# A two-layer diffusion block on one core: attention tiles in their own buffer list, the next layer's first norm chunks ahead of the context adds, and modulation bias and norm factors once per four pairs

## The chip, the cores and the metric

The kernel runs on one core of a Trainium2 chip. The metric is the device time of one execution in microseconds (us), the median of several runs; lower is better. The core has five engines with queues of their own: TensorE (PE) multiplies matrices into PSUM, VectorE (DVE) and ScalarE (ACT) do element-wise work, GpSimd (POOL) a part of it, and SyncE (SP) issues nearly all transfers from HBM.

## The reference, cut to what matters

Two layers work on 512 latent tokens (x) and 256 context tokens (h), both 1024 wide. Every layer computes a modulation from the condition vectors, normalises, projects once into four groups of mixers, projects back, and runs a SwiGLU network. `mod_c` is the same modulation from the context's condition vector.

```python
for l in range(DEPTH):                                    # DEPTH = 2
    mod = split(silu(c) @ w_mod[l] + b_mod[l], 6)         # shift1, scale1, gate1, shift2, scale2, gate2
    hn = rms_norm(h, g_norm1[l]) * (1 + mod_c[1]) + mod_c[0]
    xn = rms_norm(x, g_norm1[l]) * (1 + scale1) + shift1
    p = xn @ w_in[l]                                      # q, k, v, Fourier, convolution, pooling columns
    attn = attend(q, concat(kc, k), concat(vc, v))        # context keys come from hn
    mix = concat(attn, fourier, conv, pool) @ w_out[l]
    x = x + gate1 * mix
    xn = rms_norm(x, g_norm2[l]) * (1 + scale2) + shift2
    a, g = split(xn @ w_ffn_in[l], 2)
    x = x + gate2 * (silu(a) * g) @ w_ffn_out[l]
    # the context stream h does the same, in the first layer alone
```

## The kernel before

Activations stand transposed: `x[k]` is chunk k of the 1024 features (128 partitions) by 768 tokens, LAT (columns 0 to 511) and CTX (512 to 767). Every number is cut into a rounded high part and a rest, so that a product takes three matmuls (`mm3`: high by high, high by rest, rest by high). The cut of a weight is an ACT copy (`hi`) and a subtraction (`sub_lo`) on the engine in `lo_eng`: POOL in the mixing phase, DVE in the SwiGLU phase.

Buffers come from lists. `W` is a list of 14 tiles of 4 KB for a partition (pool `wp`): a weight of 512 KB takes three, the raw tile, `hi` and `lo`. `AL` is a list of 28 tiles of 768 numbers (`alp`), for activations. PSUM has three lists of two (`pt`, `pf`, `pb`). A tile's transfer or first write waits until an old tile of its list has had its last reader.

The order of the instructions on an engine is not that of the source. It is fixed when the program is built, by a planner that simulates the program; what stands earlier in the source goes first among what is ready in that simulation. On the chip an engine keeps the order that it was given.

The stages, with the names that the change touches:

- `mix_phase(l)`: `norm.apply` makes the chunks of the first norm (a DVE scale `xt`, an ACT shift to `xnh`, a DVE rest `xnl`), four `wq` loads feed the q, k, v projection; then 24 attention tiles in layer 0 (16 in layer 1), with the other projections, pooling, Fourier and convolution work threaded between them by `fill`, and convolution taps on DVE (`run`, L669). `make_qT` writes `qst` and `qT` (from AL), `Tile.flip` transposes a tile's probabilities into `pt_`, which two heads share (one or two W tiles).
- `mod_pairs` is a generator that runs beside the attention tiles (q 8 to 23, that is chunks 16 to 47) and, for layer 1's q 0 to 7, beside layer 0's SwiGLU. For a pair of chunks it multiplies (`mod`), copies (`me`), transposes (`mods`), reduces (L343), adds the bias (L344) and, for the scale chunks, makes the norm factor `a` (L324, `scaled_gain`).
- Out-projection at the end of `mix_phase`: eight `wo` loads; the first four are held for two passes, the last four for the first and the second part of the tokens. Meanwhile the second norm's first part is made.
- `ffn(l)`: 22 columns of 128. Layer 0 works with the seven products of a scheme of Strassen's kind (`fast`, weights by `load_ff`: two raw tiles and seven cut ones of W), after `fast_first`, which does columns 0 and 1 directly: `z` 0 is the first 384 tokens, `z` 1 the rest, whose operands `A.second` makes meanwhile. Layer 1 uses plain products (`first_step`, `ag`). `out_step` is the second matrix with its add to `x` (L1362). In the last step of layer 0 the order in the source is LAT's two `out_step`s, LAT's `n1.rstd`, CTX's two `out_step`s, CTX's `n1.rstd`; then the modulation generator is run to its end, and layer 1 begins.

Of the kernel before, what the change touches and what calls it, by code (L numbers as in the profile page):

```python
# [19 lines left out]
P = 128  # L20
# [30 lines left out]
def kernel(ctx: ExitStack, tc: tile.TileContext, xT, ctxT, vec, cst, dft,  # L51
# [8 lines left out]
    wp = ctx.enter_context(tc.tile_pool(name="wp", bufs=14))  # L60
# [16 lines left out]
    def W(name, dt=F32R):  # L77
        return wp.tile([P, 1024], dt, tag="w", name=name)

    def RAW(name):  # L80
        return W(name, F32)
# [147 lines left out]
    def load_ff(l, c):  # L229

        raws = []
        for o in (0, DFF):
            raw = RAW("ff")
            nc.sync.dma_start(out=raw.rearrange("p (a b) -> p a b", b=P), in_=rows(w_ffn_in[l][:, o + P * c:o + P * c + P]))
            raws.append(raw)
        a1, a2, g1, g2 = (r[:, 512 * i:512 * i + 512] for r in raws for i in range(2))
        ops = {}

        def cut(nm, full):
            w = ops[nm] = W("f" + nm)  # L240
            hi, lo = w[:, 0:512], w[:, 512:1024]
            act.copy(out=hi, in_=full)  # L242
            sub_lo(lo_eng[0], lo, full, hi)

        def comb(out, in0, in1, op):
            sum_eng[0].tensor_tensor(out=out, in0=in0, in1=in1, op=op)  # L246
        cut("a11", a1)
        cut("a12", a2)
        cut("a22", g2)
        comb(g2, g1, g2, ALU.add)  # L250
        comb(g1, a1, g1, ALU.subtract)
        comb(a1, g2, a1, ALU.subtract)
        comb(a2, a2, a1, ALU.subtract)
        for nm, full in (("s2", a1), ("s3", g1), ("s1", g2), ("s4", a2)):
            cut(nm, full)
        return ops
# [69 lines left out]
    def mod_pairs(l, q0, q1, mix=True):  # L326
# [11 lines left out]
        def finish(q, me):  # L338
            ps = PF("mods")
            for c in range(2):  # L340
                tr(ps[:, 128 * c:128 * c + 128], me[:, 128 * c:128 * c + 128], ident)
            m2 = modT[l][:, 2 * q:2 * q + 2, :]
            dve.tensor_reduce(out=m2, in_=ps[:, 0:256].rearrange("p (c g w) -> p c w g", c=2, g=4)[:, :, 0:2, :], axis=AX.X, op=ALU.add)  # L343
            dve.tensor_tensor(out=m2, in0=m2, in1=vcol(l, V_BM + 2 * q, 2).unsqueeze(2).to_broadcast([P, 2, 2]), op=ALU.add)  # L344
            if q // 4 in (1, 4):
                scaled_gain(l, q // 12, 2 * q % 8, 2 * q % 8 + 2)
# [252 lines left out]
    def mix_phase(l, norm, A, filler):  # L599
# [363 lines left out]
        def make_qT(i):  # L963
            j, o = qpos(i)
            st = AL("qst")
            src = qsb[j][:, o:o + 256].rearrange("p (h d) -> p h d", h=4)
            sv = lambda a: a[:, 0:512].rearrange("p (h s d) -> p h s d", h=4, s=2)
            act.copy(out=sv(st)[:, :, 0, :], in_=src)
            dve.tensor_tensor(out=sv(st)[:, :, 1, :], in0=src, in1=sv(b32(st[:, 0:512]))[:, :, 0, :], op=ALU.subtract)
            ps = PT("qT")  # L970
            for h in range(NQ):
                tr(ps[:, P * h:P * h + P], b32(st[:, P * h:P * h + P]), ident)
            qTs[i] = AL("qT")
            act.copy(out=qTs[i][:, 0:512], in_=ps[:, 0:512])

        class Tile:
# [24 lines left out]
            def flip(self, pt_):  # L1001

                e = self.h % 2
                for j, (c0, n) in enumerate(((0, 2),) if self.nk == 2 else ((0, 4), (4, 2))):
# [3 lines left out]
                    dst = pt_[j][:, 512 * e:512 * e + P * n]  # L1008
# [4 lines left out]
                if not e:  # L1013
                    return
                po = PT("pv")
                for c in range(self.nk):
                    v = vsb[:, P * (self.k0 + c) + 64 * self.kv:P * (self.k0 + c) + 64 * self.kv + 64]
                    for g in range(2):
                        o = 512 * g + P * (c % 4)
                        mm(po[64 * g:64 * g + 64, 0:P], v, pt_[c // 4][:, o:o + P], start=c == 0, stop=c == self.nk - 1,  # L1020
                           tile_position=(0, 64 * g))
# [87 lines left out]
        pt_ = None  # L1109
        for i in range(len(tiles) + 2):  # L1110
# [4 lines left out]
            if i >= 2:  # L1115
                t = tiles[i - 2]
                if t.h % 2 == 0:
                    pt_ = [W("pt", F32) for _ in range(1 if t.nk == 2 else 2)]
                t.flip(pt_)
# [84 lines left out]
    def ffn(l, norm, first, second, A, filler):  # L1204
# [22 lines left out]
        def fast_first():  # L1227
# [4 lines left out]
            for z in range(2):  # L1232
# [6 lines left out]
                for k in range(KD):  # L1239
                    if z:  # L1240
                        nm = ("b12", "b22")[k // 4]
                    else:
                        nm = ("b11", "b21")[k // 4]
                    xh, xl = A.h(nm, k % 4), A.l(nm, k % 4)
                    for i in range(4):
                        mm3(out[i], ws[i][0][:, P * k:P * k + P], ws[i][1][:, P * k:P * k + P], xh, xl, k == 0, k == KD - 1)
# [42 lines left out]
        def fast_steps():  # L1289
            fast_first()  # L1290
            for s in range(1, ns):
# [7 lines left out]
                if fin:  # L1299
                    wl = [need(("fo", l, NF - 2)), need(("fo", l, NF - 1))]  # L1300
                    for sl, st in streams:
                        out_step(s - 1, sl, st, wo, False)
                        out_step(s, sl, st, wl, True)
                        if not last:
                            n1.rstd(sl)
                else:
# [4 lines left out]
                next(filler, None)  # L1311

# [59 lines left out]
        ns = NF // 2  # L1372
        if FAST[l]:
            fast_steps()
        else:
            first_step()
# [29 lines left out]
        return n1  # L1406
# [21 lines left out]
    for l in range(DEPTH):  # L1428
        nxt = mix_phase(l, norm, A, mod_pairs(l, 8, 24))
        filler = mod_pairs(1, 0, 8, False) if l == 0 else iter(())  # L1430
        norm, A = ffn(l, *nxt, filler), None
# [82 lines left out]
```

## Time and profile before

| | us |
|---|---|
| median of three runs | 1476.47 |
| their lowest and highest | 1474.70, 1476.76 |
| the profiled execution: its own time | 1474.25 |
| its span, first to last instruction | 1472.5 |

The profiled execution lies 2.22 us under the median of the runs, and 1.75 us of its time lie around its span. The columns of a view stand in the line above its rows; times of a row are us from the span's start unless it says otherwise. "PE ssq L161 <- POOL acca L437" reads: a matmul that writes `ssq`, issued by line 161, waited for POOL's write of `acca` in line 437. Line 161 is a helper that issues all matmuls, line 105 one that issues all subtractions of cuts.

### The profile page before, as it was taken

The page shows a single profiled execution, that of the slowest core. Times are in us where ns is not written, and L with a number is a line of the kernel's source. Part 1 is how long each engine was busy: PE and PEld are TensorE (multiplying, and loading weights), DVE is VectorE, ACT ScalarE, POOL GpSimd, SP SyncE. Part 2 cuts the span into 40 slices and gives each one's busy share as a digit, 9 for nine tenths or more (in the row PEclk, how much of TensorE's full clock was granted, in tenths as well). Part 3 has the DMA queues.
Part 4 walks back from the last instruction along what each step waited for, and adds up shares of the span by engine and source line. Part 5 has one row for each costly group of instructions (what it writes and reads, how often), then busy time and mean ns, then how long its engine had stood idle before and what let it go on. Part 6 is the DMA issues. An engine that isn't in the chain of part 4 may idle for free.

```text
span 1472.5 us, 20702 instructions
## 1 busy us (share of the span) xinstructions
PE 1417.3 (96%) x8298; PEld 1217.2 (83%) x8298; DVE 945.2 (64%) x1572; ACT 600.2 (41%) x1035; POOL 199.3 (14%) x161
## 2 busy tenths in 40 slices
PE   7999988999999999999999989999899999999998
PEld 4787766998998999999999968776698888888887
DVE  3569577247986778686877777866545545444444
ACT  4457656436533233332332345666544322222220
POOL 2526420420000000000000035430240000000000
PEclk9999989999999999999999999999999999999999
DMA  9525433320323133222322233356442323333231
GB/s 297 164 87 165 157 110 107 109 71 26 104 70 103 54 91 114 87 68 76 115 86 58 92 111 92 117 169 211 127 114 80 108 86 90 111 101 100 89 98 57
DMA packets 192928, 157.35 MB, mean 107 GB/s; under 512 B 6464, under 2 KB 179520, under 8 KB 192832
## 3 DMA queue, kind: packets, MB, share of 16 engines
q1 hardware_dynamic: 192544, 155.34, 34.4%
q8 instruction: 65, 1.06, 0.3%
q10 hardware_dynamic: 288, 0.69, 0.1%
q14 instruction: 31, 0.25, 0.1%
HBM read 151.81 MB, written 4.19 MB: 106 GB/s over the span
## 4 chain that ended last, share of the span: by engine, by line
PE 83%; DVE 7%; ACT 4%; DMA 4%; issue 1%; POOL 1%; SPq 0%; ACTq 0%; DVEq 0%; POOLq 0%
PE ag L161 35%; PE fo L161 20%; PE wo L161 6%; PE qkv L161 4%; PE cv L161 3%; PE agl L161 3%; PE mod L161 3%; DVE run L669 3%; PE u L161 2%; PE ssq L161 1%; PE S L161 1%; DMA wm<-in_w_mod_dram 1%; PE pv L161 1%; PE PT L167 1%; PE cc L161 1%
## 5 line engine op out<-in xcount | busy, mean ns | idle before, releaser
L1362 DVE SCALAR_TENSOR_TENSOR x<-fo,mod,x 128x512 f32<-128x512 f32 (+1 forms) x264 | 170.7, 657 | 81.0 <-PE fo L161 80.5
L161 PE MATMUL fo<-hl,foh 128*128 128x512 f32 (+1 forms) x528 | 187.7, 356 | 0.0
L161 PE MATMUL fo<-hh,fol 128*128 128x512 f32 (+1 forms) x528 | 187.4, 356 | 0.0
L161 PE MATMUL fo<-hh,foh 128*128 128x512 f32 (+1 forms) x528 | 185.5, 358 | 1.9 <-DVE x L1362 1.4
L161 PE MATMUL ag<-t,fs 128*128 128x384 f32 x720 | 136.6, 336 | 0.9 <-DVE hg L1266 0.9
L161 PEld LDWEIGHTS ag<-t,fs 128*128 128x128 f32 x720 | 125.0, 188 | 6.4 <-issue 1.6
L161 PEld LDWEIGHTS fo<-hh,foh 128*128 128x128 f32 x528 | 99.0, 188 | 16.1 <-DVE x L1362 1.8
L161 PEld LDWEIGHTS fo<-hh,fol 128*128 128x128 f32 x528 | 99.2, 188 | 15.1 <-issue 0.2
L161 PEld LDWEIGHTS fo<-hl,foh 128*128 128x128 f32 x528 | 99.2, 188 | 14.7 <-issue 0.7
L182 ACT CAST foh<-fo 128x1024 fp32r<-128x1024 f32 x44 | 46.2, 1050 | 146.0 <-DMA fo<-in_w_ffn_out_dram 146.0
L161 PE MATMUL ag<-b,fa 128*128 128x384 f32 x480 | 92.6, 336 | 1.5 <-DVE ht L1216 1.5
L105 DVE TENSOR_TENSOR fol<-fo,foh 128x1024 fp32r<-128x1024 f32 x44 | 53.8, 1222 | 54.1 <-ACT foh L182 41.9
L669 DVE SCALAR_TENSOR_TENSOR run<-glu,vt,run 128x512 f32<-128x512 f32 (+1 forms) x98 | 87.0, 887 | 1.0
L161 PEld LDWEIGHTS ag<-b,fa 128*128 128x128 f32 x480 | 83.4, 188 | 3.4 <-DVE ht L1216 1.8
L242 ACT CAST fs<-ff 128x512 fp32r<-128x512 f32 x80 | 45.4, 620 | 75.0 <-DVE ff L246 53.0
L437 POOL TENSOR_TENSOR acca<-acca,sq 128x512 f32<-128x512 f32 (+1 forms) x4 | 4.5, 1117 | 523.8 <-ACT sq L436 523.8
L161 PE MATMUL wo<-mxh,wol 128*128 128x384 f32 (+2 forms) x224 | 73.7, 330 | 0.0
L161 PE MATMUL wo<-mxl,woh 128*128 128x384 f32 (+2 forms) x224 | 73.5, 329 | 0.0
L161 PE MATMUL wo<-mxh,woh 128*128 128x384 f32 (+2 forms) x224 | 73.5, 331 | 0.1
L161 PE MATMUL ag<-xfh,fah 128*128 128x512 f32 (+1 forms) x192 | 71.3, 376 | 1.2 <-ACT xfh L465 1.2
L161 PE MATMUL ag<-xfl,fah 128*128 128x512 f32 (+1 forms) x192 | 71.6, 373 | 0.8 <-DVE xfl L466 0.8
L242 ACT CAST fa<-ff 128x512 fp32r<-128x512 f32 x60 | 35.6, 619 | 90.2 <-PE ag L161 51.7
(319 smaller groups left out, 3308.1 us busy)
## 6 DMA issues: line engine op xcount, KB each, us to landing
wm<-in_w_mod_dram SPq DMA_DIRECT2D x64, 512.0 KB, 4.4
fo<-in_w_ffn_out_dram SPq DMA_DIRECT2D x44, 512.0 KB, 3.3
ff<-in_w_ffn_in_dram SPq DMA_DIRECT2D x40, 512.0 KB, 4.7
fa<-in_w_ffn_in_dram SPq DMA_DIRECT2D x24, 512.0 KB, 4.4
fg<-in_w_ffn_in_dram SPq DMA_DIRECT2D x24, 512.0 KB, 3.9
wm<-in_w_mod_dram SPq DMA_DIRECT2D x40, 256.0 KB, 5.3
wo<-in_w_out_dram SPq DMA_DIRECT2D x16, 512.0 KB, 4.8
wm<-in_w_mod_dram SPq DMA_DIRECT2D x16, 384.0 KB, 3.3
```

What stands on the lines that cost most here:

```text
L105: eng.tensor_tensor(out=out, in0=full, in1=b32(hi), op=ALU.subtract)
L161: i = last_pe[0] = pe.matmul(*a, **kw)
L167: i = last_pe[0] = pe.transpose(*a)
L182: act.copy(out=hi[:, :n], in_=raw[:, :n])
L242: act.copy(out=hi, in_=full)
L437: eng.tensor_tensor(out=a, in0=a, in1=t[:, sl], op=ALU.add)
L669: yield dve.scalar_tensor_tensor(out=cacc[b][:, :cwid] if j == CONVW - 1 else run, in0=glu[b][:, j:j + cwid], scalar=tap(b, j), in1=cacc[b ...
L1362: dve.scalar_tensor_tensor(out=x[m][:, sl], in0=ps[:, :n], scalar=modT[l][:, 40 + m, st:st + 1], in1=x[m][:, sl], op0=ALU.mult, op1=ALU.add)
```

## The change

1. W has 11 tiles instead of 14. A new list `AT` has four tiles of 768 numbers, which is the same memory. From it come `qst`, `qT`, and a tile `pt` for each head (before: `pt_` from W for two heads, `qst` and `qT` from AL), and in `load_ff` the raw weights, now four loads of 512 numbers a partition instead of two of 1024.
2. The bias add and the norm factor of the modulation are done once for eight chunks (every fourth q), not for each pair.
3. In `fast_first`, `z` 1 does the four outputs in two passes of two over all eight k, not all four for each k.
4. In the last step of layer 0, behind LAT's `n1.rstd` and ahead of CTX's `out_step`s in the source, the modulation generator is run to its end, and layer 1's first norm is applied to chunks 0 and 1 of LAT.

```diff
-    wp = ctx.enter_context(tc.tile_pool(name="wp", bufs=14))
+    wp = ctx.enter_context(tc.tile_pool(name="wp", bufs=11))
+    tp = ctx.enter_context(tc.tile_pool(name="tp", bufs=4))
...
+    def AT(name, dt=F32):
+        return tp.tile([P, T], dt, tag="at", name=name)
...
-        for o in (0, DFF):
-            raw = RAW("ff")
-            nc.sync.dma_start(out=raw.rearrange("p (a b) -> p a b", b=P), in_=rows(w_ffn_in[l][:, o + P * c:o + P * c + P]))
+        for o, i in ((0, 0), (0, 1), (DFF, 1), (DFF, 0)):
+            raw = AT("ff")[:, 0:512]
+            nc.sync.dma_start(out=raw.rearrange("p (a b) -> p a b", b=P), in_=rows(w_ffn_in[l][512 * i:512 * i + 512, o + P * c:o + P * c + P]))
             raws.append(raw)
-        a1, a2, g1, g2 = (r[:, 512 * i:512 * i + 512] for r in raws for i in range(2))
+        a1, a2, g2, g1 = raws
...
-            m2 = modT[l][:, 2 * q:2 * q + 2, :]
-            dve.tensor_reduce(out=m2, in_=ps[:, 0:256].rearrange("p (c g w) -> p c w g", c=2, g=4)[:, :, 0:2, :], axis=AX.X, op=ALU.add)
-            dve.tensor_tensor(out=m2, in0=m2, in1=vcol(l, V_BM + 2 * q, 2).unsqueeze(2).to_broadcast([P, 2, 2]), op=ALU.add)
-            if q // 4 in (1, 4):
-                scaled_gain(l, q // 12, 2 * q % 8, 2 * q % 8 + 2)
+            dve.tensor_reduce(out=modT[l][:, 2 * q:2 * q + 2, :], in_=ps[:, 0:256].rearrange("p (c g w) -> p c w g", c=2, g=4)[:, :, 0:2, :],
+                              axis=AX.X, op=ALU.add)
+            if q % 4 == 3:
+                v = modT[l][:, 2 * q - 6:2 * q + 2, :]
+                dve.tensor_tensor(out=v, in0=v, in1=vcol(l, V_BM + 2 * q - 6, KD).unsqueeze(2).to_broadcast([P, KD, 2]), op=ALU.add)
+                if q // 4 in (1, 4):
+                    scaled_gain(l, q // 12, 0, KD)
...
-            st = AL("qst")
+            st = AT("qst", F32R)
...
-            qTs[i] = AL("qT")
+            qTs[i] = AT("qT", F32R)
...
-            def flip(self, pt_):
+            def flip(self, pair):
...
+                self.pt = AT("pt")
...
-                    dst = pt_[j][:, 512 * e:512 * e + P * n]
+                    dst = self.pt[:, P * c0:P * (c0 + n)]
...
-                for k in range(KD):
...
-                    for i in range(4):
-                        mm3(out[i], ws[i][0][:, P * k:P * k + P], ws[i][1][:, P * k:P * k + P], xh, xl, k == 0, k == KD - 1)
+                for pair in ((0, 1), (2, 3)) if z else ((0, 1, 2, 3),):
+                    for k in range(KD):
+                        nm = f"b{1 + k // 4}{1 + z}"
+                        for i in pair:
+                            mm3(out[i], ws[i][0][:, P * k:P * k + P], ws[i][1][:, P * k:P * k + P], A.h(nm, k % 4), A.l(nm, k % 4),
+                                k == 0, k == KD - 1)
...
                         if not last:
                             n1.rstd(sl)
+                            if st == 0:
+                                for _ in filler:
+                                    pass
+                                nxt = Acts("xn")
+                                for k in range(2):
+                                    n1.apply(l + 1, 0, k, sl, st, nxt)
...
-        norm, A = ffn(l, *nxt, filler), None
+        norm, A = ffn(l, *nxt, filler)
```

## Rows read from the trace of the kernel before

**Rows 1.** The page's first part: busy us (share of the span) and instructions.

```profile
PE 1417.3 (96%) x8298; PEld 1217.2 (83%) x8298; DVE 945.2 (64%) x1572; ACT 600.2 (41%) x1035; POOL 199.3 (14%) x161
```

**Rows 2.** Busy time by stretch: engines (instructions), granted PE clock, DMA share, GB/s.

```profile
160.00:262.00 102.00, 88.44 (x704) 69.39 (x705) 66.38 (x143) 61.14 (x137) 13.43 (x14) 0.90 0.39 119
389.00:837.00 448.00, 447.15 (x2615) 416.74 (x2614) 345.59 (x605) 143.86 (x254) 0.00 (x0) 1.00 0.28 85
1139.00:1446.00 307.00, 307.00 (x1345) 252.16 (x1344) 145.03 (x167) 81.02 (x95) 0.00 (x0) 1.00 0.31 95
```

**Rows 3.** PE's waits, 837 to 890: total us, times, longest us.

```profile
PE ssq L161 <- POOL acca L437: 4.0, 1, 4.0
PE fo L161 <- DVE x L1362: 1.4, 1, 1.4
```

**Rows 4.** PE's waits, 340 to 390.

```profile
PE ag L161 <- DVE b L105: 1.7, 2, 1.0
PE ag L161 <- DVE ht L1216: 1.5, 1, 1.5
```

**Rows 5.** The chain that ended last, 100 to 270: start, us, what.

```profile
126.44 1.60 DVE mod L344
131.14 1.70 DVE mod L344
153.53 1.58 DVE mod L344
```

**Rows 6.** Busy time of L344's bias adds alone, on DVE, 75 to 262.

```profile
75.00:262.00 187.00, 8.57 (x16) 0.95 0.39 123
```

**Rows 7.** Timeline near 131, DVE and then POOL: start, us, instruction.

```profile
130.10 1.04 DVE L669 SCALAR_TENSOR_TENSOR run<-glu,vt,run 128x783 f32<-128x783 f32 x1
131.05 1.79 DVE L344 TENSOR_TENSOR mod<-mod,vt 128x4 f32<-128x4 f32 x1
...
130.95 1.88 POOL L685 TENSOR_TENSOR ca<-ca,prod 128x783 f32<-128x783 f32 x1 [0.57 <-ACT prod L684]
```

**Rows 8.** The chain that ended last, 925 to 1110 (layer 1's mixing phase).

```profile
957.96 0.80 DVE mod L344
```

**Rows 9.** The chain that ended last, 837 to 893.

```profile
878.46 3.68 PE ssq L161 x8
...
882.36 5.47 PE qkv L161 x24
```

**Rows 10.** Timeline at the layers' boundary, DVE and then POOL.

```profile
864.85 3.35 DVE L451 RECIPROCAL R<-R 128x512 f32<-128x512 f32 x1
868.12 1.95 DVE L1362 SCALAR_TENSOR_TENSOR x<-fo,mod,x 128x256 f32<-128x256 f32 x5
...
877.74 1.87 DVE L463 SCALAR_TENSOR_TENSOR xt<-x,a,R 128x512 f32<-128x512 f32 x2
879.86 3.18 DVE L466 SCALAR_TENSOR_TENSOR xnl<-xt,mod,xnh 128x512 fp32r<-128x512 f32 x2 [0.24 <-ACT xnh L465]
...
869.14 2.40 POOL L105 TENSOR_TENSOR wql<-wq,wqh 128x1024 fp32r<-128x1024 f32 x1 [12.12 <-PE fo L161]
...
879.28 2.55 POOL L105 TENSOR_TENSOR wcl<-wc,wch 128x1024 fp32r<-128x1024 f32 x1 [0.88 <-ACT wch L182]
```

**Rows 11.** All engines' busy time in one stretch, columns as in the second group.

```profile
878.60:882.00 3.40, 3.40 (x9) 2.58 (x10) 3.15 (x3) 1.84 (x3) 2.55 (x1) 0.50 0.00 0
```

**Rows 12.** The chain that ended last, 318 to 392.

```profile
364.01 16.40 PE ag L161 x92
```

**Rows 13.** The chain that ended last, 1060 to 1125.

```profile
1093.71 5.31 DMA fg<-in_w_ffn_in_dram
...
1099.09 1.06 ACT fgh L182
...
1100.18 1.23 DVE fgl L105
```

**Rows 14.** SP's waits, 290 to 390.

```profile
SPq L188 <- PE wo L161: 31.3, 3, 23.0
```

More of the change, by code (lines that the diff above doesn't have):

```diff
@@ L999, in soft @@
                 act.activation(out=pr[:, 0:kw], in_=pr[:, 0:kw], func=AF.Copy, scale=st[:, 2:3])
-            def flip(self, pt_):
-                e = self.h % 2
+            def flip(self, pair):
+                self.pt = AT("pt")
                 for j, (c0, n) in enumerate(((0, 2),) if self.nk == 2 else ((0, 4), (4, 2))):
@@ L1012, in flip @@
                         act.copy(out=dst, in_=pt[:, 0:P * n])
-                if not e:
+                if self.h % 2 == 0:
                     return
@@ L1018, in flip @@
                     for g in range(2):
-                        o = 512 * g + P * (c % 4)
-                        mm(po[64 * g:64 * g + 64, 0:P], v, pt_[c // 4][:, o:o + P], start=c == 0, stop=c == self.nk - 1,
+                        mm(po[64 * g:64 * g + 64, 0:P], v, pair[g].pt[:, P * c:P * c + P], start=c == 0, stop=c == self.nk - 1,
                            tile_position=(0, 64 * g))
@@ L1108, in mix_phase @@
         pull(pace.taps0)
-        pt_ = None
         for i in range(len(tiles) + 2):
@@ L1115, in mix_phase @@
             if i >= 2:
[L1116 to L1119, printed above, removed]
+                tiles[i - 2].flip(tiles[i - 3:i - 1])
             fill(pace.fill * (1 - pace.share))
@@ L1238, in fast_first @@
                     A.second(norm, l, second)
-                for k in range(KD):
[L1240 to L1244, printed above, removed]
-                    for i in range(4):
-                        mm3(out[i], ws[i][0][:, P * k:P * k + P], ws[i][1][:, P * k:P * k + P], xh, xl, k == 0, k == KD - 1)
+                for pair in ((0, 1), (2, 3)) if z else ((0, 1, 2, 3),):
[4 more added lines that the diff above has]
+                                k == 0, k == KD - 1)
                 for c in range(2):
@@ L1289, in fast_steps @@
         def fast_steps():
+            nxt = None
             fast_first()
@@ L1311, in fast_steps @@
                 next(filler, None)
+            return nxt
         def first_step():
@@ L1372, in ffn @@
         ns = NF // 2
+        nxt = None
         if FAST[l]:
-            fast_steps()
+            nxt = fast_steps()
         else:
@@ L1405, in ffn @@
             pass
-        return n1
+        return n1, nxt
     lo_eng[0] = pool
```

## The prediction

> **What bounds the kernel now.** I read the page first: PE is busy for 1417.3 of 1472.5 us [rows 1], so only what idles PE, slows it, or holds the queue in front of it can move the time. The busy time by stretch then says where that is. Both SwiGLU stretches are full: 0.85 us of 448 are idle in layer 0 and nothing of 307 in layer 1 [rows 2]. The second half of layer 0's mixing phase is not: 13.56 us of 102 are idle, at a mean granted clock of 0.90 [rows 2]. The rest is at the seams, which PE's waits show: 4.0 and 1.4 us at the boundary of the layers [rows 3], 3.2 us in `fast_first` [rows 4]. In the mixing phase PE's own waits are many and small, so there I read the chain that ended last. Between 122 and 160 it is nearly all DVE, and three of its longer pieces are the bias adds that the change thins out [rows 5].
>
> **The bias adds and norm factors.** Twelve of sixteen bias adds a layer go, and as many norm factors out of each four but one. A bias add writes 4 numbers a partition, but the sixteen in layer 0 took 8.57 us [rows 6]. The timeline says why: the add at 131.05 lasted 1.79 us and ended at 132.84, and POOL's add of 1.88 us, begun at 130.95, ended at 132.83. The tap ahead of it, which reads its running sum from PSUM, took 1.04 us as usual [rows 7]. So the add waited for POOL, the tap did not. Three such adds are on the chain, 1.60 + 1.70 + 1.58 = 4.88 us [rows 5]; by source order they belong to q 8, 9 and 12, which no longer add. The next instruction on DVE is mostly a tap, or a reduction out of PSUM, so the wait should not pass on to it.
>
> Bounds: below, nothing, if PE sets the pace there after all; above, the whole 8.57. I take 3.9, four fifths of what is on the chain, because behind it lie 13.56 us of idle PE into which the taps' earlier end can be passed on [rows 2]. In layer 1 one add of 0.80 us is on the chain [rows 8]; I take 0.7, between 0 and 0.80. What is late next in both is PE's threaded work. The eight-chunk add and factor come later for the first pairs of a group, but their readers (gates in the out-projection, `a` in the second norm) stand behind all q: no cost. If that cover were gone, it would be one add, up to 1.79 us [rows 7].
>
> **The boundary of the layers.** Before, PE ran out of work behind CTX's last `fo` matmul and waited 4.0 us for POOL's sum of squares, which CTX's norm needs [rows 3]; then came 3.68 us of its eight `ssq` matmuls, and only then 24 matmuls of layer 1's first two chunks, 5.47 us [rows 9]. Nothing in those 24 needs CTX. With the chunks made ahead they can fill the hole. Against this stands DVE's queue: LAT's reciprocal holds it for 3.35 us to 868.20, which costs PE 1.4 us already, since CTX's adds free PE's PSUM tiles [rows 3, 10]. Ahead of these adds now come two `xt` (1.87 us) and, when ACT has made the high parts, two `xnl` (3.18 us) [rows 10]; besides them the last pair's reduction and one add.
>
> I reckon that the two `xt` lengthen PE's short wait by 1.87 us while the hole of 4.0 closes: 2.1 won. PE's granted clock was 0.50 from 878.6 to 882.0, the lower level of 1.2 GHz, after that idle time [rows 11]. Without the hole the `ssq` matmuls may run at 2.4 GHz, half of 3.68, so 1.84 more. Between 2.1 and 2.1 + 1.84 I take 3.1. Bounds: 4.0 + 1.4 + 1.84 = 7.2 won if both waits and the slow clock go; 1.87 + 3.18 + 2.40 - 4.0 = 3.5 lost if the adds stand behind all four chunk operations and one POOL subtraction [rows 10].
>
> This last is a mechanism that the rows show: the two `xnl` at 879.86 took 3.18 us while POOL's subtraction of 2.55 us ran from 879.28 [rows 10], and at the new place another of 2.40 us stands at 869.14. The Trainium skill, SBUF — State Buffer, section "Who interferes with whom", has the rule: a DVE instruction with two SBUF inputs and a GpSimd instruction that reads SBUF shut each other out, and whichever starts first keeps the other waiting to its end. The bias adds agree, at 1.79 us beside POOL's 1.88. By the rule the chunk operations, which have two SBUF inputs, are exposed at the new place, and CTX's adds with one are not, but queue behind them: it speaks against this part, and the rival on POOL below gives its time.
>
> **The two passes in `fast_first`.** No matmul is added. A pass over two outputs uses up a chunk in 6 matmuls instead of 12, at 16.40 / 92 = 0.178 us each [rows 12], so 1.07 us instead of 2.14, and PE had waited twice for chunks at the old pace (1.7 us, `b`) [rows 4]. So the first pass is likely to wait more, and the second not at all. Matmuls of the next column's products can stand in. Bounds: 3.2 won (all of rows 4), 4.3 lost (half of a pass of 48 matmuls, 8.5). I take 0.5 lost.
>
> **Eleven weight tiles.** At the end of the out-projection four `wo` weights hold eight W tiles. Six were left, enough for three cut weights; three are left now, one cut weight and one raw. In layer 1 the fourth SwiGLU weight was on the chain already: its transfer began at 1093.71, when PE released `wo` tiles, and took 5.31, its cut 1.06 and 1.23 us [rows 13]. Now the third and fourth both wait for PE. Bounds: nothing, if PE does the first two outputs meanwhile; 5.31 + 1.06 + 1.23 = 7.60 if a whole load is added. I take 1.5, nearer to the lower end, as half of the matmuls need only the first two weights. In layer 0 the same wait was 23.0 us long on SP [rows 14] with first tokens that are longer; I take 0.5, bounds 0 and 7.60.
>
> **At nothing.** The attention tiles' copies and matmuls stay as they are. A q takes six AT tiles (`qst`, `qT`, four `pt`) from a list of four; the fifth replaces `qst` and the sixth `qT`, whose last readers stand ahead on PE, since a flip comes two tiles behind its scores. Without this cover, 0.1 us at 40 flips would be 4.0. In the SwiGLU stretches the raw weights have tiles of their own now: two raw tiles of fourteen before, so twelve for cut weights and `fo`, against eleven. Twenty more pairs of issues go to SP, behind which `fo` and `wm` transfers queue; SP waits longest for tiles, not for its issues [rows 14]. The cover is that PE idles only 0.85 us there [rows 2]; without it, one more wait of that size in each of ten steps would cost 8.5. Fewer AL tiles are asked for: no gain that a row shows.
>
> **Sum.** -3.9 - 0.7 - 3.1 + 0.5 + 1.5 + 0.5 = -5.2. The profiled execution took 1474.25 us, so 1469.05; on the median of the runs, 2.22 us higher, 1471.3.
>
> **Rivals.**
> - *PE sets the pace.* DVE's saving in the mixing phases is not passed on, since PE is busy for most of them; the first two terms vanish. -0.6, so 1475.9. For it: PE is at 88.44 of 102 [rows 2]. Against: the chain goes through the adds [rows 5].
> - *POOL shuts the moved chunks out.* The 2.40 us of `wql` and the stretch of `xnl` over `xt`, 3.18 - 1.87 = 1.31 [rows 10], fall on the queue in front of CTX's adds: 3.7 of the boundary's gain go. -1.5, so 1475.0. Against: where that subtraction stands depends on when `wq`'s tiles come free.
> - *The weight list decides* (the other side). In both first SwiGLU steps a whole load of 7.60 us [rows 13] comes late and PE has nothing to put in its place: +15.2 in place of +2.0, so +8.0 and 1484.5. It makes the kernel slower by over 0.2% from a cost of lists of some 10.2. For it: a W wait already ends on the chain [rows 13]. Against: PE's matmuls of the first two outputs.
> - *All gains come.* 4.88 + 0.80 + 7.2 with no loss from lists or passes: -12.9, so 1463.6.
>
> **Chances.** 0.2% of the time, 3.0 us, is about what a measurement can tell from no change. Forecast 0.45 and all gains 0.13: faster 0.58. PE's pace 0.14 and POOL 0.10: same 0.24. The weight list 0.18: slower. The likeliest one's own range is 1467 to 1473.5. For 8 in 10 the range goes to 1462, below the best case, and to 1481, which takes in the milder half of the weight list.
>
> **What would show it.** L344 with four adds a layer, in layer 0 under 1.5 us together, and PE's idle time between 160 and 262 smaller than 13.56. At the boundary, `qkv` matmuls ahead of the last `ssq`, no wait of 4.0 for `acca`, no stretch at clock 0.50 there; a PE wait for `x` over 3.3 or long `xt` would speak for POOL. Waits of PE for `fa` or `fg` cuts at either first step, of over 2 us, or idle PE in the two full stretches, would speak for the weight list. I am wrong if the mixing phases come out longer: the planner places everything there anew, and this I cannot see from the trace.

## The result, and the profile after

The changed kernel takes 1485.81 us (median of 4 runs, 1483.86 to 1488.56), the kernel before 1475.59 beside it (4 runs): a ratio of 1.0068, 95% interval 1.0054 to 1.0082. So it is 10 us slower; I had forecast 1471.3, with 1462 to 1481 for 8 in 10, and 0.58 for faster. The profiled execution took 1485.75 us with a span of 1484.0.

The first part of the page, for [rows 1]:

```profile
PE 1426.5 (96%) x8298; PEld 1223.0 (82%) x8298; DVE 932.7 (63%) x1533; ACT 598.4 (40%) x1034; POOL 198.4 (13%) x161
```

The 39 instructions fewer on DVE are there, and 12.5 us less of its time. PE does the same 8298 matmuls in 9.2 us more, at a mean granted clock of 0.982 for 0.990.

The busy time by stretch, for [rows 2], moved with the work:

```profile
159.00:262.00 103.00, 92.24 (x751) 73.58 (x744) 59.41 (x115) 57.23 (x130) 21.50 (x18) 0.95 0.51 156
388.00:829.00 441.00, 440.89 (x2607) 414.37 (x2606) 341.44 (x594) 141.20 (x252) 0.00 (x0) 1.00 0.28 84
1150.00:1457.00 307.00, 307.00 (x1344) 252.02 (x1344) 144.25 (x167) 81.92 (x95) 0.00 (x0) 1.00 0.32 96
```

The SwiGLU stretches are full as before. The second half of layer 0's mixing phase, where I saw the gain, has 10.76 us idle for 13.56, and yet the layer's first `ag` matmul starts 1.4 us later than before (337.75 for 336.31).

Where the time goes can be told by work done instead. Both traces hold all 8298 matmuls, so the end of the n-th one can be set side by side. The order differs between the kernels, so n marks an amount of work and not one matmul. The first two rows stand at the start of layer 0's SwiGLU and behind its last `ag`.

| n | before, us | changed, us | difference |
|---|---|---|---|
| 2066 | 336.76 | 337.56 | +0.80 |
| 5002 | 847.08 | 841.99 | -5.09 |
| 5200 | 891.02 | 888.70 | -2.32 |
| 5350 | 920.42 | 918.12 | -2.30 |
| 5400 | 931.29 | 937.80 | +6.51 |
| 5500 | 951.81 | 961.37 | +9.56 |
| 8298 | 1468.55 | 1480.04 | +11.49 |

So the changed kernel wins 5.9 us in layer 0's SwiGLU, gives 2.8 back at the boundary, loses 8.8 between its 5350th and its 5400th matmul, 3.1 more in the next hundred, and 1.9 from there to the end. The win belongs to the lists: from the 2066th to the 5002nd matmul the nine executions with eleven weight tiles and attention tiles (this one and eight of the experiments below) take 504.1 to 506.3 us, the ten with the old loads 509.8 to 510.9. By kind the matmuls of this stretch are the same to within a few. PE's idle time makes up 2.1 us of the 5.9; what the rest is, and whether the raw tiles of their own or the half loads bring it, is not shown. PE's waits at the boundary and in layer 1's first projection, 858 to 892 and then 892 to 930 (total us, times, longest):

```profile
PE ssq L165 <- ACT sq L425: 2.2, 1, 2.2
PE cv L165 <- ACT wch L186: 1.5, 1, 1.5
PE fo L165 <- DVE x L1369: 1.3, 1, 1.3
PE qkv L165 <- ACT xnh L471: 1.2, 1, 1.2
...
PE cv L165 <- ACT glu L767: 5.5, 1, 5.5
```

The wait of 4.0 for `acca` [rows 3] is gone as forecast. That for `x` is 1.3 for 1.4; the three others, 4.9 us together, are new, and so is the one of 5.5. The clock, for [rows 11], over the three half-speed stretches of this place:

```profile
878.30:888.50 10.20, 7.46 (x19) 5.08 (x18) 8.58 (x12) 4.61 (x8) 3.84 (x2) 0.50 0.18 54
922.70:929.50 6.80, 5.38 (x13) 4.22 (x14) 3.96 (x9) 4.71 (x7) 1.75 (x1) 0.50 0.75 233
943.20:950.00 6.80, 5.91 (x18) 4.64 (x19) 4.33 (x7) 5.67 (x9) 2.69 (x3) 0.50 0.18 64
```

Before, one stretch of 3.4 us stood here [rows 11]. Now 23.8 us are granted 0.50, the lower level of 1.2 GHz, and each of the three follows idle time of PE (2.2 us; 5.5; 2.2 at 940); the waits of 1.5 and 1.2 lie inside the first. PE is busy for 18.75 us of the three, for 3.40 before; at full speed these would be half, so I estimate that 7.7 of the 9.2 us by which PE's busy time grew come from here. Not every wait has this price: before, PE waits 2.3 us for `S` at 936, and the clock stays at 1.00 behind it (this wait, and the clock of 933 to 950):

```profile
PE S L161 <- ACT K L736: 2.3, 1, 2.3
```

```profile
933.00:950.00 17.00, 14.06 (x82) 10.57 (x81) 11.99 (x19) 14.34 (x23) 11.32 (x10) 1.00 0.34 107
```

ACT's timeline around the wait of 5.5 shows its cause (start, us, instruction, idle time before it and its releaser):

```profile
911.19 1.05 ACT L186 CAST wch<-wc 128x1024 fp32r<-128x1024 f32 x1 [6.51 <-DMA wc<-in_w_in_dram]
...
918.60 1.04 ACT L186 CAST wih<-wi 128x1024 fp32r<-128x1024 f32 x1 [4.07 <-PE cv L165]
919.55 0.26 ACT L646 COPY ksb<-qkv 128x128 f32<-128x128 f32 x1
...
922.17 1.28 ACT L767 ACT_TABLE_LOAD   x1
923.47 0.60 ACT L767 ACTIVATE glu<-cv 128x512 f32<-128x512 f32 x1
```

PE's `cv` matmul at 924.12 waits for a `glu` that empties its PSUM tile. But `glu` was not slow: ahead of it on ACT's queue stood a cut of the next weight, `wih`, which found a tile only when the `cv` matmuls that ended at 918.58 let one go. For 4.07 us ACT could do nothing, with all the work for PE behind. This is the weight list, at a place that I had not looked at. The wait of 2.2 at 875 is of the same kind: PE's `ssq` waits for ACT's `sq`, behind a cut whose raw came late:

```profile
876.31 1.04 ACT L186 CAST wqh<-wq 128x1024 fp32r<-128x1024 f32 x1 [4.82 <-DMA wq<-in_w_in_dram]
877.26 0.72 ACT L425 ACTIVATE sq<-x 128x256 f32<-128x256 f32 x2
```

PE's waits in `fast_first`, for [rows 4], and the four bias adds of layer 0, for [rows 6]:

```profile
PE ag L165 <- DVE b L109: 1.7, 2, 0.9
```

```profile
75.00:262.00 187.00, 0.85 (x4) 0.97 0.46 141
```

PE's waits from 1044 to 1150, with layer 1's first SwiGLU step (before, the two were 1.2 and 0.8):

```profile
PE ag L165 <- ACT xfh L471: 2.5, 1, 2.5
...
PE ag L165 <- DVE xfl L472: 0.9, 1, 0.9
```

### The profile page after: what moved, and what is told of

It reads as the page before. It is cut to its first block, busy times and chain, and to the rows that moved or that the text cites. A ratio compares the mean times of both kernels' runs of the same rounds, so it can differ in the third digit from the quotient of the medians.

```text
span 1484.0 us, 20772 instructions
## 1 busy us (share of the span) xinstructions
PE 1426.5 (96%) x8298; PEld 1223.0 (82%) x8298; DVE 932.7 (63%) x1533; ACT 598.4 (40%) x1034; POOL 198.4 (13%) x161
## 5 line engine op out<-in xcount | busy, mean ns | idle before, releaser
L165 PE MATMUL ag<-xfh,fal 128*128 128x512 f32 (+1 forms) x192 | 72.1, 376 | 0.0
L186 ACT CAST fgh<-fg 128x1024 fp32r<-128x1024 f32 x24 | 25.2, 1050 | 115.3 <-DMA fg<-in_w_ffn_in_dram 64.7
```

The source lines that it names most:

```text
L165: i = last_pe[0] = pe.matmul(*a, **kw)
L186: act.copy(out=hi[:, :n], in_=raw[:, :n])
```

## The experiments

My first theory after the result was the short list alone; the rivals were each of the other parts. All ratios are to the kernel before, run on the same chip, with 95% intervals.

| run | median us | ratio | interval |
|---|---|---|---|
| list_alone | 1477.95 | 1.0017 | 1.0001 to 1.0033 |
| early_alone | 1478.12 | 1.0019 | 1.0007 to 1.0030 |
| bias_alone | 1482.27 | 1.0046 | 1.0031 to 1.0060 |
| pass_alone | 1475.37 | 0.9998 | 0.9989 to 1.0006 |
| all_but_list | 1478.84 | 1.0020 | 1.0011 to 1.0029 |
| all_but_early | 1483.00 | 1.0053 | 1.0039 to 1.0068 |
| all_but_bias | 1480.68 | 1.0037 | 1.0023 to 1.0051 |
| bias_in_mix_only | 1474.64 | 0.9993 | 0.9985 to 1.0002 |
| first_raws_in_AT | 1478.65 | 1.0019 | 1.0010 to 1.0028 |
| twelve_tiles_only | 1482.38 | 1.0041 | 1.0027 to 1.0055 |
| early_two_no_drain | 1481.65 | 1.0039 | 1.0026 to 1.0052 |
| early_four_no_drain | 1485.71 | 1.0066 | 1.0052 to 1.0080 |
| raws_in_AT_no_grouping | 1474.18 | 0.9988 | 0.9979 to 0.9996 |
| mended_without_early | 1478.74 | 1.0015 | 1.0005 to 1.0025 |
| grouped_in_mix_and_passes | 1474.95 | 0.9993 | 0.9984 to 1.0003 |
| raws_in_AT_grouped_in_mix | 1477.83 | 1.0016 | 1.0007 to 1.0024 |
| raws_in_AT_lists_and_passes | 1473.39 | 0.9990 | 0.9981 to 0.9999 |

One execution of the kernels with short lists says less than one of before: `list_alone` ranged from 1473.50 to 1486.81 over 12 runs, and its profiled execution was the slowest of them. So sizes are taken from the ratios, places from the profiles.

### Each part alone

Each is the kernel before with the hunks of one part of the diff, whole: `list_alone` with those of the lists (pools, `load_ff`, `make_qT`, `flip`), `early_alone` with those in `fast_steps` and `ffn`, `bias_alone` with that in `finish`, `pass_alone` with that in `fast_first`. Their first lines, in this order:

```diff
-    wp = ctx.enter_context(tc.tile_pool(name="wp", bufs=14))
+    wp = ctx.enter_context(tc.tile_pool(name="wp", bufs=11))
+    tp = ctx.enter_context(tc.tile_pool(name="tp", bufs=4))
...
+                            if st == 0:
+                                for _ in filler:
...
+            if q % 4 == 3:
+                v = modT[l][:, 2 * q - 6:2 * q + 2, :]
...
+                for pair in ((0, 1), (2, 3)) if z else ((0, 1, 2, 3),):
```

> The kernel before with the lists alone changed: eleven weight tiles, four attention tiles, four half loads a SwiGLU column. If the shorter weight list is what costs, this run alone is 8 to 12 us slower than before (1.0055 to 1.008), with PE waits for weights at layer 1's first projection (some 5 us for a convolution weight) and a first SwiGLU step of layer 1 that begins 8 to 11 us late. If the early norm chunks are the cause, it is within 3 us of before.

> The kernel before with layer 1's first two norm chunks made ahead of the context adds, and nothing else. By the theory of the short list it gains what was forecast at the boundary, 0 to 4 us (ratio 0.997 to 1.000), and the half-clock stretch at the boundary is at most as long as before (3.4 us). If the early chunks are the cause of the loss, since qkv matmuls then come before their weights, it is 5 to 10 us slower, with two or more stretches at half clock between 860 and 950.

> The kernel before with the bias adds and norm factors once per four pairs, and nothing else. By the forecast's term 3.9 + 0.7 us faster (0.9969); if PE sets the pace in the mixing phases, within 1 us of before; if the new placement of layer 0's convolution (whose last chunk came 21 us later in the changed kernel) comes from here, the attention ends some 12 us earlier and the out-projection no earlier, so a gain of 0 to 1 us.

> The kernel before with the context half of layer 0's first SwiGLU step in two passes of two outputs, and nothing else. Forecast 0.5 us slower, bounds 3.2 faster and 4.3 slower; PE's waits for the second half's chunks were 3.2 us before and 1.7 us in the changed kernel, so 1 to 2 us faster (0.999) if nothing else moves.

The theory of the list alone fell: the dearest part by itself is the grouping, 6.6 us, the one that I had put at 4.6 us of gain. Most of its loss has one place, PE's waits from 862 to 892:

```profile
PE qkv L161 <- ACT xnh L467: 5.1, 1, 5.1
PE ssq L161 <- POOL acca L439: 4.0, 1, 4.0
PE fo L161 <- DVE x L1364: 1.4, 1, 1.4
```

The last two stood there before [rows 3]. The first is new, and DVE's timeline with one row of POOL's shows what it hangs on:

```profile
881.97 0.18 DVE L342 TENSOR_REDUCE mod<-mods 128x4 f32<-128x16 f32 x1 [4.88 <-PE mods L167]
882.18 0.17 DVE L346 TENSOR_TENSOR mod<-mod,vt 128x16 f32<-128x16 f32 x1
882.27 1.74 DVE L453 RECIPROCAL R<-R 128x256 f32<-128x256 f32 x1
883.93 1.46 DVE L324 SCALAR_TENSOR_TENSOR a<-mod,vt 128x16 f32<-128x16 f32 x1
885.50 2.20 DVE L465 SCALAR_TENSOR_TENSOR xt<-x,a,R 128x512 f32<-128x512 f32 x4
...
883.02 2.34 POOL L105 TENSOR_TENSOR wcl<-wc,wch 128x1024 fp32r<-128x1024 f32 x1 [2.14 <-ACT wch L182]
```

Layer 1's chunk 0 needs its norm factor `a`. Before, chunks 0 and 1 had theirs with pair q 4; grouped, the factor of all eight chunks comes with pair 7, whose transposes stand on PE behind the context's `ssq`. So `xt` starts at 885.50, where before its first two started at 877.74 [rows 10], and the 24 `qkv` matmuls that covered the context norm have nothing to read. The factor itself, 16 numbers a partition, took 1.46 us and ended at 885.39, as POOL's subtraction ended at 885.36: the mechanism of [rows 7] again.

The early chunks alone lose 2.5 to 2.8 us instead of gaining 3.1; the lists alone 2.3; the passes nothing. The lists' 2.3 us are a balance: from the 2066th to the 5002nd matmul `list_alone` takes 504.8 us for 510.3 before, and loses more than that win further on. Its wait is in its profile, 900 to 930, and 7.4 us long there; before, no such wait stands:

```profile
PE cv L165 <- ACT glu L765: 7.4, 1, 7.4
```

The expectations call it a wait for a convolution weight; by the releaser it is one for `glu`, behind a cut for which there is no tile or no raw yet, as shown above.

### Each part taken out, and grouping without the boundary

Three are the changed kernel with the hunks of one part undone: the lists, the early chunks with the draining, the grouping. The fourth is the kernel before with the grouping under one more condition:

```diff
+            if mix and q % 4 == 3:
+                v = modT[l][:, 2 * q - 6:2 * q + 2, :]
...
+            if mix:
+                return
```

> The changed kernel with the old lists (fourteen weight tiles, no attention tiles, two raw loads a column). Theory A: grouping the norm factors made layer 1's first chunks wait for the last modulation pair, which ends behind the context adds (5.1 us of idle PE at 882 in the run with the bias adds alone); here the pairs are drained ahead of the context adds, so that wait is gone, and what is left of the loss in the changed kernel is the short weight list: this run is within 3 us of before (1.000 to 1.002). Theory B, that the costs of the parts add up (6.6 for the bias adds, 2.4 for the early chunks): 1.006.

> The changed kernel without the early norm chunks and without the early draining of the modulation pairs. Theory A: layer 1's first qkv matmul waits again for the last pair's factor, a PE wait of 4 to 6 us near 880, but the convolution weights win that time, so their wait near 918 (5.5 us in the changed kernel) shrinks: 1.004 to 1.007, about as the changed kernel. Theory B, costs add up: 6.6 + 2.3 = 8.9 us, 1.006.

> The changed kernel with a bias add and a norm factor for every pair again. Theory A: with the pairs drained early, grouping costs nothing in the changed kernel, so taking it out leaves the loss: 1.005 to 1.007, with the wait for a convolution weight near 918 still there. Theory B: the loss falls to 2.3 + 2.4 = 4.7 us, 1.003.

> The kernel before with one bias add and one factor per four pairs only for the pairs that are worked off in the two mixing phases; layer 1's first eight pairs, worked off in layer 0's SwiGLU, keep one add a pair and their factors. Theory A: the wait of 5.1 us at layer 1's first qkv matmul is gone, and 0.5 to 1.5 us are won in layer 0, as in the run with the bias adds alone ahead of 860: 0.999 to 1.000. If the grouping costs through the new placement in the mixing phases, 1.003 to 1.005 as there.

Theory A held in three of four, though the ratio of `all_but_early` fits theory B too; its waits speak for A, 4.2 us for layer 1's first chunk and 3.1 for `glu`. With the grouping kept off the eight pairs that end at the boundary, its loss is gone (0.9993 for 1.0046), and PE waits only as before:

```profile
PE ssq L161 <- POOL acca L444: 4.0, 1, 4.0
PE fo L161 <- DVE x L1369: 1.4, 1, 1.4
```

With the pairs drained early and the old lists, grouping costs nothing more (`all_but_list` 1.0020, early chunks alone 1.0019), so the 1.0068 falls by 0.0048 when only the lists go back: some 7 us for the list in company, 2.3 alone, both net of the win in layer 0's SwiGLU. `all_but_bias` missed: grouping still costs 0.0031 in the changed kernel, which theory A had at nothing. With 0.0015 for the early chunks, within the noise, the three parts taken out one by one come to more than the 0.0068 that they cost together.

### The list's wait, mended and dosed

In the changed kernel, layer 1's raw `wq` and `wc` halves go into attention tiles, unused at that time, so that the eleven weight tiles hold cuts alone; the work is the same, in more and shorter cuts. The other kernel is before with twelve weight tiles.

```diff
+            hi, lo = W(name + "h"), W(name + "l")
+            for i in range(2):
+                raw = AT(name)[:, 0:512]
+                nc.sync.dma_start(out=raw, in_=src[:, i, :])
+                act.copy(out=hi[:, 512 * i:512 * i + 512], in_=raw)
...
-    wp = ctx.enter_context(tc.tile_pool(name="wp", bufs=14))
+    wp = ctx.enter_context(tc.tile_pool(name="wp", bufs=12))
```

> The changed kernel, with the raw halves of layer 1's qkv and convolution weights in attention tiles, which nobody uses there, so that the eleven weight tiles hold cut weights alone at that place; more, shorter cuts (two of 512 columns instead of one of 1024). If the short weight list costs by layer 1's first projection, PE's wait for a convolution weight near 918 (5.5 us) falls under 2 us and its wait of 2.2 us for the squares near 875, behind a late cut on ACT, goes; the ratio falls from 1.007 to 1.002 to 1.004. If the list costs somewhere else, 1.006 to 1.008 with the waits gone; if it isn't the list, the waits stay.

> The kernel before with twelve weight tiles instead of fourteen, nothing else (the attention's pt stay among them). By the list theory a dose between none and that of the run with the lists alone: a PE wait of 1 to 5 us for a convolution weight near 918, where before has none and the lists alone have 7.4; ratio 1.000 to 1.003. If the wait belongs to the four half loads or the attention tiles, none there.

The mend gives 1.0019, all that giving the old lists back gives. The wait of 5.5 is gone from PE's waits (900 to 930), for ACT's cut found its raw and its tile at 912.66:

```profile
PE cv L165 <- DVE glu L789: 0.3, 1, 0.3
```

```profile
912.66 1.05 ACT L186 CAST wih<-wi 128x1024 fp32r<-128x1024 f32 x1
...
916.20 0.60 ACT L788 ACTIVATE glu<-cv 128x512 f32<-128x512 f32 x1
```

Twelve tiles miss: 1.0041, and no wait for `cv` in 900 to 945. So two tiles fewer cost more than the whole of the lists in `list_alone`. Part of it is that nothing is won in layer 0's SwiGLU: from the 2066th to the 5002nd matmul this kernel takes 510.9 us, as before. `pt` still draws on the shorter list too; where that costs, its profile doesn't settle (it took 1479.67, under its median).

### The early chunks, without the drain and with four

Both are `early_alone` without its draining; the second also with four chunks:

```diff
-                                for _ in filler:
-                                    pass
...
-                                for k in range(2):
+                                for k in range(4):
```

> The kernel before with layer 1's first two chunks ahead of the context adds, the modulation pairs drained at the old place. Theory: the 24 matmuls that fill the hole were the cover of the next wait, for the context norm's reciprocal and the chunk operations behind it, so 3 us of idle PE stand behind them as in the run with the early chunks alone (1.14 + 2.01): 1.001 to 1.003. If instead the draining cost, at most 1.000.

> As the last, with four chunks made early. If what was missing is cover, the second 24 matmuls take the place of the first and the idle time behind the hole falls from 3 to under 1.5 us: 0.998 to 1.000. If the adds queue behind the chunk operations on DVE, PE's waits for x near 865 rise over 3 us in all: 1.002 to 1.005.

More chunks cost more: 1.0039 and 1.0066. Neither stated reason fits as put: PE's waits for `x` stay at 1.4 and 1.8. What moved is the end of the context's part. With four, the last `fo` matmul ends 9.30 us later than before and the last `ssq` 7.74. Before, the context's adds follow one another from 868.12 on [rows 10]; now DVE's timeline, and a row of POOL's, are:

```profile
867.66 1.56 DVE L1368 SCALAR_TENSOR_TENSOR x<-fo,mod,x 128x256 f32<-128x256 f32 x4
869.14 4.48 DVE L463 SCALAR_TENSOR_TENSOR xt<-x,a,R 128x512 f32<-128x512 f32 x4
873.54 1.25 DVE L1368 SCALAR_TENSOR_TENSOR x<-fo,mod,x 128x256 f32<-128x256 f32 x3
874.72 2.29 DVE L466 SCALAR_TENSOR_TENSOR xnl<-xt,mod,xnh 128x512 fp32r<-128x512 f32 x1
876.94 0.47 DVE L1368 SCALAR_TENSOR_TENSOR x<-fo,mod,x 128x256 f32<-128x256 f32 x1
...
874.07 2.39 POOL L105 TENSOR_TENSOR wql<-wq,wqh 128x1024 fp32r<-128x1024 f32 x1 [2.80 <-DMA wc<-in_w_in_dram]
```

The chunk operations stand among the context's adds, and the `qkv` matmuls among its `fo` matmuls. PE stays busy, so no wait for `x` shows, but the context's norm is late. The price falls due further on: this kernel is 1.6 us ahead of before at the 5350th matmul and 8.7 behind at the 5500th, and in that stretch PE waits for the first keys and queries of layer 1's attention (`ksl` 2.3, `qst` 2.1), with 13.7 us at a granted clock of 0.50. That these are late through the context's norm is argued, not shown. One `xnl` took 2.29 us and ended at 877.01, behind POOL's subtraction at 876.46; another took 0.73 elsewhere in that timeline. The rule that the prediction took from the Trainium skill, SBUF — State Buffer, section "Who interferes with whom", that such a DVE instruction and a GpSimd one shut each other out, bore on the moved chunks as it said.

### What grouping costs with the short lists

These five combine edits shown above, with no new line. Four are `first_raws_in_AT` with the grouping hunk undone (`raws_in_AT_no_grouping`), or with the grouping under `mix` (`raws_in_AT_grouped_in_mix`), each also with the early chunks undone (`raws_in_AT_lists_and_passes`, `mended_without_early`). The fifth, `grouped_in_mix_and_passes`, is `bias_in_mix_only` with the two passes.

> The changed kernel with layer 1's qkv and convolution raws in attention tiles, and a bias add and factor for every pair again. With grouping this was 1.0019. If what grouping costs in the changed kernel goes through the short list (it does nothing where the list doesn't end the wait), the same, 1.001 to 1.003. If it is a cost of its own beside the list, 0.003 lower: 0.998 to 1.000.

> The changed kernel without the early chunks, with layer 1's qkv and convolution raws in attention tiles and grouping in the mixing phases only: the parts of the change without the two waits that the experiments found. If these two and the early chunks are all that costs, 0.998 to 1.000, with no PE wait over 2 us for a weight or a factor between 880 and 925. If the short list also costs elsewhere (out-projection, SwiGLU), 1.002 to 1.004.

> The kernel before with grouping in the mixing phases only and the two passes: old lists, no early chunks. The two alone gave 0.9993 and 0.9998; if they add up, 0.999 (0.998 to 1.000).

> The changed kernel with layer 1's first raws in attention tiles, grouping in the mixing phases only. Grouping everywhere gave 1.0019, nowhere 0.9988. If it costs in the mixing phases (layer 0's out-projection ends some 3 to 8 us later than without, with a PE wait of 3 to 4 us for pt near 248): 1.001 to 1.003. If it costs by the late factors of layer 1's first norm: 0.998 to 1.000.

> The changed kernel with layer 1's first raws in attention tiles, without the grouping and without the early chunks: the lists and the passes alone, mended. With the early chunks this was 0.9988. If these are worth something here (the weights are there earlier), 1.000 to 1.002; if they cost 0.002 as on the old lists, 0.996 to 0.998.

`mended_without_early` missed (1.0015, with 5.9 us of PE's wait for the first `xnh` at the boundary), and so did `raws_in_AT_lists_and_passes`, whose 0.9990 lies between its two ranges. With the short lists grouping costs 0.003 of its own, and it costs it in the mixing phases (1.0016 grouped there, 1.0019 grouped everywhere, 0.9988 not grouped; without the early chunks 1.0015 and 0.9990). The busy time from 159 to 330 (PE, PEld, DVE, ACT, POOL) of three ungrouped executions (the two `raws_in_AT`, `list_alone`), then three grouped ones (changed, `first_raws_in_AT`, `raws_in_AT_grouped_in_mix`):

```profile
159.00:330.00 171.00, 161.84 (x1158) 140.49 (x1157) 95.94 (x191) 91.18 (x185) 43.92 (x29) 0.97 0.40 119
```

```profile
159.00:330.00 171.00, 161.10 (x1150) 139.28 (x1149) 95.28 (x190) 91.74 (x186) 42.72 (x28) 0.97 0.40 119
```

```profile
159.00:330.00 171.00, 158.43 (x1135) 136.12 (x1132) 88.08 (x177) 84.06 (x171) 43.48 (x30) 0.95 0.38 113
```

```profile
159.00:330.00 171.00, 157.20 (x1100) 134.56 (x1093) 85.51 (x164) 83.34 (x171) 41.35 (x28) 0.95 0.38 114
```

```profile
159.00:330.00 171.00, 156.97 (x1102) 133.91 (x1101) 83.26 (x163) 83.95 (x170) 41.71 (x28) 0.95 0.37 113
```

```profile
159.00:330.00 171.00, 156.53 (x1098) 133.82 (x1094) 84.64 (x163) 83.10 (x171) 41.45 (x28) 0.95 0.38 114
```

Ungrouped, PE gets through 1135 to 1158 matmuls there (before: 1104), grouped through 1098 to 1102 (in `all_but_bias` 1135, in the two grouped ones not shown 1103 and 1115). A count in a fixed stretch flatters a kernel that comes late into it: `list_alone` ends its 2066th matmul at 339.4, later than the changed kernel (337.56). The two ungrouped `raws_in_AT` end it at 331.1 and 330.5, the same two with grouping in the mixing phases at 337.9 and 339.4. These differences, 6.8 and 9.0 us, are about those at the last matmul, 7.2 and 8.4 (the medians differ by less, 0.0028 and 0.0025 of the time): so layer 0's mixing phase is the place. All ungrouped short-list kernels have the same order of matmuls in this layer; the grouped ones leave it at the 753rd. At the end of the phase PE and ACT, in the changed kernel (the other grouped ones wait 2.7 to 4.2 us for `pt`):

```profile
PE pv L165 <- ACT pt L1018: 3.5, 1, 3.5
```

```profile
247.56 1.04 ACT L186 CAST woh<-wo 128x1024 fp32r<-128x1024 f32 x1 [4.63 <-DMA wo<-in_w_out_dram]
248.52 0.39 ACT L959 ACTIVATE mxh<-fo 128x256 fp32r<-128x256 f32 x1
248.80 0.36 ACT L1018 COPY pt<-PT 128x256 f32<-128x256 f32 x1
```

Once more a cut that waits for its raw weight stands on ACT ahead of what PE needs. In the ungrouped order (`raws_in_AT_no_grouping`) the cut stands ahead of `pt` too (246.76 and 247.99), but PE has other matmuls until 248.33 there. That this wait and the later LayerNorm (1.9 us of PE's time at `lnB`) are the whole 0.003 is not shown: the ungrouped executions wait too, 0.3 to 3.6 us, at a `mod` matmul near 250.

Two kernels have intervals below 1, both ungrouped with the raws in attention tiles: 0.9988 with the early chunks, 0.9990 without. That is 1.5 to 1.8 us, under the 0.2% of the prediction's bound, and the early chunks bring nothing there that could be told.

## Why the prediction was wrong, point by point

Two terms carry the miss: the weight tiles, put at +2.0, cost some 7 us (0.0048 goes with them), and the grouping, put at -4.6, costs some 4.6 (0.0031). With the list's wait mended and the grouping undone, nothing of the loss is left (0.9988).

- **Bias adds** (-3.9 - 0.7): the mechanism was right and the gain absent. Four adds take 0.85 us where sixteen took 8.57 (that the tap beside one of them didn't wait [rows 7] was no test, as it began 0.85 us ahead of POOL's add), but on the old lists this is worth 0.0007 of the time, about 1 us, not to be told from nothing: the rival that PE sets the pace. The step that failed is "their readers ... stand behind all q: no cost". It holds in the mixing phases; at the boundary the reader, layer 1's chunk 0, stands right behind pair 7. The price without cover, "one add, up to 1.79 us", was wrong as well: 5.1 us of wait and 6.6 us in all, since the cover of the next norm went with it. In the changed kernel the early draining hides this, and grouping costs 0.003 in the mixing phases instead.
- **Boundary** (-3.1): measured +2.5 to +2.8 alone. The hole of 4.0 closed, as forecast, and PE's wait for `x` did not grow by the 1.87 that I had put against it (1.3 for 1.4). But "Nothing in those 24 needs CTX. With the chunks made ahead they can fill the hole" overlooked that the 24 matmuls already covered the context norm's reciprocal and first chunks. Ahead of it they left that uncovered; `early_alone` waits, 862 to 892:

```profile
PE qkv L161 <- ACT xnh L465: 2.0, 1, 2.0
PE cv L161 <- ACT R L450: 1.1, 1, 1.1
```

These 3.1 us for 4.0 explain why almost nothing was won, not why time was lost. Against before, `early_alone` gains 1.1 us from the 5002nd to the 5200th matmul and loses 3.4 from there to the 5500th, at the first keys of layer 1's attention, where PE waits 4.1 us for 2.9 and 3.4 us run at 0.50. Why that stretch got longer stays open. The upper bound of +3.5 held.
- **Passes** (+0.5): -0.0002, nothing; the waits for `b` are 1.7 for 1.7; that for `ht` (1.5) is gone in the changed kernel and in `list_alone`, not in the passes alone, so the lists took it away.
- **Eleven weight tiles** (+2.0): the size at the first SwiGLU step of layer 1 was about right (2.5 and 0.9 us of waits for 1.2 and 0.8). The step that failed is that I looked for the price only there. It was paid at layer 1's first projection, where eight `wq` cuts and eight `wc` cuts, sixteen tiles, pass through the list: 2.3 us alone, some 7 in the changed kernel, net. In layer 0's first step, put at +0.5, PE's waits fell from 3.2 to 1.7 us. The rival "the weight list decides" gave the time (1484.5) by luck: its price was to fall in the two first SwiGLU steps.
- **Attention tiles at nothing**: for the attention not contradicted; of the ungrouped short-list executions `list_alone` ends layer 0's mixing phase 2.6 us later than before, the three others 1.6 to 6.3 earlier. For the SwiGLU stretches a gain was put at nothing: I weighed the raw weights' own tiles for a loss alone, because "PE idles only 0.85 us there" [rows 2]. They gave 4 to 6 us in layer 0's SwiGLU in every execution with the short lists, and only 2.1 of the 5.9 in the changed kernel were idle time of PE: a PE that shows as busy can still be held up.
- **New placement**: the prediction ended on it as what it could not see, and gave it no chance. It goes with the 0.003: the grouped kernels have another order of matmuls and end layer 0's mixing phase later. That the order is the cause, and not the later adds themselves, is not shown.

## What to carry to other kernels

When an update is batched, look for the earliest reader of the first item against the last producer of the batch, across phase boundaries too: here one batch in ten had such a reader, and by itself it cost 6.6 us, where all the others saved about 1. Before a tile list is shortened, count its tiles at every place where it is the clock of loads, and look at what stands behind a cut on the same in-order engine. Matmuls that could fill a hole earlier are often already filling one: name the next wait that they leave bare. And compare kernels by the time at which the same amount of work is done: busy shares near 100% hid a win of some 5 us here.

## What was not expected of the hardware

An engine's queue passes a late weight on to work that doesn't need it: ACT's cut of `wih` waited 4.07 us for a tile, and PE 5.5 us for a `glu` that reads no weight. And after such waits PE's granted clock was 0.50 for 10.2, 6.8 and 6.8 us at this place, for 3.4 before, so that by my estimate 7.7 us of PE's busy time were added with the same matmuls. A wait of 2.3 us before had no such stretch behind it, one of 2.2 us in the changed kernel had 6.8 us: what decides between them is not shown.
